# First blocks row by row in written order, residual transposes ahead of norm 2's rows, and a halved last head

## The chip, the cores and the metric

The kernel runs on one core of a Trainium2 chip. The metric is the device time of one execution in microseconds. Engines are named as in the profile: PE (matrix), PEld (its weight loads), DVE (vector), ACT (scalar), POOL, and SP, which only issues DMAs.

## The reference, cut to what matters

A block of a streaming encoder on 512 tokens of width 1024, in float32: an adaptive vector from `c`, a mixer on a normed and modulated input, and a channel sub-layer that retrieves 16 of 16,384 experts for each of 8 heads.

```python
c_act = jax.nn.silu(c)
ada = c_act @ w_ada[l] + b_ada[l]
sh1, sc1, g1, sh2, sc2, g2 = jnp.split(ada, 6, axis=-1)
h = modulate(rmsnorm(x, norm1_g[l]), sh1, sc1)      # h * (1 + scale) + shift
z = h @ w_in[l]                                     # 1024 -> 2560
...                                                 # convolutions and RG-LRU on z
y = jnp.concatenate([head_rmsnorm(y_a, ...), head_rmsnorm(y_b, ...)], axis=-1) @ w_out[l]
x = x + g1[:, None, :] * y
h = modulate(rmsnorm(x, norm2_g[l]), sh2, sc2)
x = x + g2[:, None, :] * peer(h, w_q[l], sub_keys[l], expert_u[l], expert_v[l])
return rmsnorm(x, final_g)
```

`peer` forms `q = h @ w_q`, scores it against 128 keys on each of two halves, takes the top 16 of each and of their sums, and weighs the chosen experts' outputs.

## The kernel before

Everything up to the experts lies transposed: features on partitions, in eight rows of 128 (`xs[:, k, :]`, k = 0 to 7), and 512 tokens along the free axis. A product with a weight matrix goes block by block, 128 output features at a time. Each float32 weight block is split into a high part (`high`, an ACT copy, L76) and a low part (`low`, a DVE subtraction, L81), the modulated input likewise (L214, L215), and `mm3` adds three matmuls for each of the eight rows: high by high (L90), high by low (L91), low by high (L92). A block is thus 24 matmuls into one PSUM tile.

The front. ACT squares the eight rows (L159, L162), DVE adds them up in `sqa` (L164), one set of matmuls with `ones` sums over partitions (`stat`, L154), DVE and ACT form `rstd` (`rsqrt_small`, L111 to L117), and `rows_of` (L172) spreads it over partitions in `ps_rs`. The first third of the adaptive vector comes in four quarters (`ada_quarter`): four loads of 512 KB each (L190), four pieces of matmuls each (L192) into `ps_g`, an ACT copy `row` (L195), two transposes by the identity (L198), and small DVE additions (L203 to L205) that leave shift and scale `A` for two rows. Then these two rows are modulated. `row` 7 is ready only after the fourth quarter. The softplus of `lam` is a run of small DVE operations (L234 to L254). The bulk of the front is not written in order: a scheduler places the instructions on each engine.

The mixer has 20 input blocks in the list `order`; `zblock` loads, splits and multiplies one, and after each block takes one step of `ada_rest`, whose steps are groups of matmuls L134 for the rest of the adaptive vector. The recurrent branch multiplies `xc` with the block-diagonal `bd` (cleared at L261; L331, L333). Blocks live in the PSUM tiles `ps_z` (three buffers) and `ps_g` (two).

Eight w_out blocks follow, each ending in the residual (L388), a square, and, with the last two squares, the sums (L154). In norm 2 the new residual is also written out in token order: `x1_mm` transposes four rows of 128 tokens (L399) into `ps_z`, `x1_out` copies them to `xn` on ACT (L405; two buffers) and stores them (L406, POOL) to `x1d`. Group 0 to 2 are transposed around `rows_of`, the others one in each of the first heads of the q loop. The rows of h come from L434 (DVE), L213, L214 (ACT) and L215; `full2` transposes them too (L423, L425), into `h2n` and `h2b`.

The q loop makes one q block per head, scores it against the keys (L488) and evicts the scores `sc` (L494). On DVE the top-16 search (`early`, L451 to L460) starts with the first scores. Then the u chunks start: expert weights in blocks of 128, split by the same L76 and L81, multiplied into `ps_act` (pool `psE`). From there on the order is written out by hand, by a planner (`manual_schedule`).

Of the kernel before, what the change touches and what calls it, by code (L numbers as in the profile page):

```python
# [34 lines left out]
def block_kernel(ctx, tc, xT, small, w_ada1, w_ada, b_ada, w_in, w_r, w_i, w_out, w_q, keys, uT, u, v, final_g, out):  # L35
# [120 lines left out]

    def sq_sum(k, split):
        if k == 0:
            nc.scalar.activation(sqa, xs[:, 0, :], AF.Square)  # L159
# [25 lines left out]
    def ada_quarter(j):  # L185
        pr = psZ.tile([128, 256], F32, name="ps_g", bufs=2)
        nc.vector.memset(pr, 0.0)
        for k2 in range(4):
# [1 line left out]
            nc.sync.dma_start(wt.rearrange("p a b c -> p (a b c)"), w_ada1[4 * j + k2])  # L190
            for b in range(4):
                nc.tensor.matmul(pr[32 * b:32 * b + 1, :], cs[:, 2 * k2 + b // 2:2 * k2 + b // 2 + 1],  # L192
                                 wt[:, b // 2, b % 2, :], start=(k2 == 0), stop=(k2 == 3), skip_group_check=True)
        row = ada0.tile([128, 256], F32, name="row0", bufs=2)
        nc.scalar.activation(row, pr, AF.Copy)  # L195
        pc = psA.tile([128, 2, 128], F32, name="ps_row")
        for i in range(2):
            nc.tensor.transpose(pc[:, i, :], row[:, i * 128:(i + 1) * 128], ident)  # L198
# [6 lines left out]
        nc.vector.scalar_tensor_tensor(A1[:, ks], adac[:, 8 + 2 * j:10 + 2 * j], 1.0, sm("n1g")[:, ks],  # L205
                                       op0=OP.add, op1=OP.mult)
# [4 lines left out]
    def modulate(t1, k, A, B, hh, hl, full=None):
        f = sq_pool.tile([128, T], F32, name="mfull")
        nc.vector.tensor_scalar(f, t1, A[:, k:k + 1], B[:, k:k + 1], op0=OP.mult, op1=OP.add)  # L213
        nc.scalar.activation(hh[:, k, :], t1, AF.Identity, scale=A[:, k:k + 1], bias=B[:, k:k + 1])  # L214
# [19 lines left out]
    nc.vector.tensor_scalar(z_, lam, -1.0, None, op0=OP.mult)  # L234
    nc.vector.tensor_tensor(z_, z_, lam, op=OP.max)
    nc.scalar.activation(tn, z_, AF.Tanh, scale=1.0 / 16)
    nc.vector.tensor_scalar(e_, tn, 1.0, None, op0=OP.add)
    nc.vector.reciprocal(e_, e_)
    nc.vector.tensor_scalar(tn, tn, -1.0, 1.0, op0=OP.mult, op1=OP.add)
    nc.vector.tensor_mul(e_, e_, tn)  # L240
    for _ in range(3):
        nc.vector.tensor_mul(e_, e_, e_)
    nc.vector.tensor_scalar(w_, e_, 2.0, None, op0=OP.add)
    nc.vector.reciprocal(w_, w_)
    nc.vector.tensor_mul(w_, w_, e_)
    nc.vector.tensor_mul(w2, w_, w_)
    nc.vector.memset(ac, 1.0 / 15)
    for n in range(6, -1, -1):
        nc.vector.tensor_mul(ac, ac, w2)
        nc.vector.tensor_scalar(ac, ac, 1.0 / (2 * n + 1), None, op0=OP.add)  # L250
# [885 lines left out]
```

## Time and profile before

| | us |
|---|---|
| median of three runs | 1416.25 (1416.03, 1416.25, 1418.21) |
| the profiled execution | 1418.33 |
| its span | 1416.6 |

| engine | busy us | share of the span |
|---|---|---|
| PE | 1363.8 | 96% |
| DVE | 1241.4 | 88% |
| ACT | 753.0 | 53% |
| POOL | 497.1 | 35% |

The span runs from the first to the last instruction of the core; the time of an execution has some 2 us around it. A share over the whole span is an average over stages with different limits, so what a change is worth is read in the stage that it touches, by windows and by what each engine waited for there. In rows of instructions the first number is the start in microseconds, the second the time taken, then engine, line, operation, what is written and read, and in brackets the idle time just before with what ended it. The granted clock is that of PE: 1.00 is full speed.

### The profile page before, as it was taken

To read this page: it belongs to the slowest core of one execution; us is meant where nothing else is said; L and a number is where in the kernel's file an instruction comes from. 1 tells how busy PE (TensorE), PEld (TensorE's weight loads), DVE (VectorE), ACT (ScalarE), POOL (GpSimd) and SP (SyncE) were. 2 spreads that over 40 slices of the span, in tenths; PEclk is the share of its full clock that TensorE was granted. 3 is DMA by queue.
4 is the path that set the end of the run, shared out by engine and by line. 5 is a ranking of instruction groups with operands and counts; after the bars stand their busy time and mean duration, and the time that the engine had idled before them with its cause. 6 is when DMAs were issued, how large, how long until landed. Compare 5 with 4: busy or idle time off the path is not lost.

```text
span 1416.6 us, 22503 instructions
## 1 busy us (share of the span) xinstructions
PE 1363.8 (96%) x7739; PEld 1179.4 (83%) x7739; DVE 1241.4 (88%) x2598; ACT 753.0 (53%) x1340; POOL 497.1 (35%) x334
## 2 busy tenths in 40 slices
PE   5999998999999999999999989999999999999995
PEld 2566777779999999999999978876878888888884
DVE  6676555899999899999999967988989999999998
ACT  3554433445498699856995434343344434344442
POOL 0000000000135334415342534655656565555550
PEclk9999999999999999999999989999999999999998
DMA  9575323124689899979999999999999999999994
GB/s 381 207 271 190 119 89 100 57 83 149 213 299 387 314 354 370 388 232 323 353 374 350 339 380 354 381 372 390 391 411 410 412 409 412 405 409 409 406 370 163
DMA packets 160758, 440.13 MB, mean 311 GB/s; under 512 B 16258, under 2 KB 68482, under 8 KB 158596
## 3 DMA queue, kind: packets, MB, share of 16 engines
q1 hardware_dynamic: 113636, 267.76, 51.0%
q0 software_dynamic: 46720, 169.89, 31.3%
q8 instruction: 61, 1.00, 0.3%
q10 hardware_dynamic: 288, 1.05, 0.2%
q14 instruction: 53, 0.43, 0.1%
HBM read 393.54 MB, written 45.09 MB: 310 GB/s over the span
## 4 chain that ended last, share of the span: by engine, by line
PE 43%; issue 21%; DVE 14%; DMA 13%; POOL 6%; ACT 1%; SPq 1%; DVEq 0%; POOLq 0%; ACTq 0%
PE acc L987 18%; POOL rows L730 6%; DMA wraw<-in_v_dram 6%; PE ps_z L90 5%; PE ps_z L92 5%; PE ps_z L91 5%; DVE scr L751 3%; DMA rows<-in_u_dram,idx_s 2%; DVE wlo L81 2%; PE ps_act L90 2%; PE ps_act L92 2%; PE ps_act L91 2%; DVE cl L874 2%; DVE ys L767 1%; DMA act<-Ad 1%
## 5 line engine op out<-in xcount | busy, mean ns | idle before, releaser
L76 ACT ACTIVATE whi<-wraw 128x1024 fp32r<-128x1024 f32 x292 | 308.2, 1056 | 334.3 <-DMA wraw<-in_v_dram 131.9
L81 DVE TENSOR_TENSOR wlo<-wraw,whi 128x1024 fp32r<-128x1024 f32 x292 | 356.1, 1221 | 71.5 <-ACT whi L76 70.6
L90 PE MATMUL ps_act<-h,whi 128*128 128x320 f32 x1024 | 322.4, 315 | 1.6 <-ACT sc L494 1.2
L91 PE MATMUL ps_act<-h,whi 128*128 128x320 f32 x1024 | 317.0, 310 | 0.0
L92 PE MATMUL ps_act<-h,wlo 128*128 128x320 f32 x1024 | 316.8, 309 | 0.0
L730 POOL DMA_INDIRECT rows<-in_u_dram,idx_s x128 | 194.1, 1516 | 239.0 <-DVE scr L751 189.8
L730 POOL DMA_INDIRECT rows<-in_v_dram,idx_s x128 | 198.7, 1552 | 147.0 <-DVE ys L767 119.5
L987 PE MATMUL acc<-whi,ch 128*128 128x512 f32 x750 | 234.3, 393 | 13.0 <-ACT ch L884 6.7
L987 PE MATMUL acc<-whi,cl 128*128 128x512 f32 x750 | 234.3, 394 | 0.4
L987 PE MATMUL acc<-wlo,ch 128*128 128x512 f32 x750 | 233.2, 392 | 0.0
L90 PEld LDWEIGHTS ps_act<-h,whi 128*128 128x128 f32 x1024 | 193.1, 189 | 2.2 <-ACT sc L494 1.4
L91 PEld LDWEIGHTS ps_act<-h,whi 128*128 128x128 f32 x1024 | 193.1, 189 | 0.2
L92 PEld LDWEIGHTS ps_act<-h,wlo 128*128 128x128 f32 x1024 | 192.7, 188 | 0.0
L987 PEld LDWEIGHTS acc<-whi,ch 128*128 128x128 f32 x750 | 141.7, 190 | 44.7 <-ACT ch L884 8.4
L730 POOL DMA_INDIRECT rows<-in_u_dram,idx_b x64 | 99.1, 1548 | 211.7 <-DVE scr L751 109.1
L987 PEld LDWEIGHTS acc<-whi,cl 128*128 128x128 f32 x750 | 141.4, 190 | 33.5 <-DVE cl L874 4.6
L987 PEld LDWEIGHTS acc<-wlo,ch 128*128 128x128 f32 x750 | 142.3, 190 | 29.9
L767 DVE SCALAR_TENSOR_TENSOR ys<-rows,acts,ys 128x1024 f32<-128x1024 f32 x127 | 162.8, 1282 | 1.6
L751 DVE SCALAR_TENSOR_TENSOR scr<-rows,h2n 128x1024 f16<-128x1024 f32 x128 | 156.4, 1222 | 8.3 <-DMA rows<-in_u_dram,idx_s 6.6
L884 ACT ACTIVATE ch<-cf 128x384 fp32r<-128x384 f32 x128 | 67.3, 526 | 93.4 <-DVE cf L881 91.0
L817 ACT ACTIVATE act<-ps_act 128x320 f32<-128x320 f32 x128 | 55.5, 433 | 102.2 <-PE ps_act L92 100.3
L406 POOL DMA_DIRECT2D x1d<-xn x8 | 4.6, 578 | 281.8 <-DVE wlo L81 234.4
(258 smaller groups left out, 1964.7 us busy)
## 6 DMA issues: line engine op xcount, KB each, us to landing
wraw<-in_uT_dram SPq DMA_DIRECT2D x128, 512.0 KB, 6.5
wraw<-in_v_dram SPq DMA_DIRECT2D x128, 512.0 KB, 10.0
Gd<-stg SPq DMA_DIRECT2D x46, 512.0 KB, 6.9
wada<-in_w_ada_dram SPq DMA_DIRECT2D x16, 1024.0 KB, 5.0
Ad<-act SPq DMA_DIRECT2D x96, 160.0 KB, 7.6
act<-Ad SPq DMA_DIRECT2D x96, 160.0 KB, 11.0
h<-Gd SPq DMA_DIRECT2D x12, 1024.0 KB, 14.7
wraw<-in_w_in_dram SPq DMA_DIRECT2D x20, 512.0 KB, 5.8
```

Source lines behind the costliest of these rows:

```text
L76: nc.scalar.activation(hi, raw, AF.Copy)
L81: nc.vector.tensor_sub(lo, raw, hi.bitcast(F32))
L90: nc.tensor.matmul(ps, hi[:, k, :], xh(k), start=first and k == ks[0], stop=False)
L91: nc.tensor.matmul(ps, hi[:, k, :], xl(k), start=False, stop=False)
L92: nc.tensor.matmul(ps, lo[:, k, :], xh(k), start=False, stop=last and k == ks[-1])
L730: nc.gpsimd.indirect_dma_start(out=r[:, :], out_offset=None, in_=table, in_offset=bass.IndirectOffsetOnAxis(ap=idxs[:, k:k + 1], axis=0))
L751: nc.vector.scalar_tensor_tensor(scr, rows.pop(n), 1.0, hn, op0=OP.mult, op1=OP.mult, accum_out=dst[:, k:k + 1])
L767: nc.vector.scalar_tensor_tensor(ys, rows.pop(k), acts[:, k:k + 1], ys, op0=OP.mult, op1=OP.add)
L817: nc.scalar.activation(act[c], ps, AF.Gelu)
L874: nc.vector.tensor_sub(cl, cf, ch.bitcast(F32))
L884: nc.scalar.activation(ch, cf, AF.Copy)
L987: nc.tensor.matmul(accs[b][e], st[:, bs], mv[:, e * 512:(e + 1) * 512], start=first, stop=last)
```

## The change

It has three places. **The front** is put under a written order. The loads come in the order of `FW`. Squares are formed in `xn1`, added in pairs and summed pair by pair. The first quarter of the vector is worked off at once; the pieces of the other three stand in the table `ADA` between matmuls of the blocks. Of the vector's row only the needed columns are picked out, by a matmul with two columns (`selc`) in place of two transposes. The first four blocks no longer run one after the other: for each row k, one of the three products is added in all four blocks, then the next. Softplus is a generator that is advanced between the rows. Blocks 4 and 5 are split between the blocks' last rows.

```diff
+    for what in FW:
+        if what[0] == "p":
+            ada_load(int(what[1]))
+        else:
+            raws[order[int(what[1])]] = load_w(w_in[order[int(what[1])]])
...
+    for k in range(0, KB, 2):
+        for i in range(2):
+            nc.scalar.activation(xn1[:, k + i, :], xs[:, k + i, :], AF.Square)
+        nc.vector.tensor_add(xn1[:, k, :], xn1[:, k, :], xn1[:, k + 1, :])
+        stat(xn1[:, k, :], k == 0, k == KB - 2)
+    for i in range(4):
+        ada_mm(0, i)
+    rstd1 = const.tile([128, NT], F32, name="rstd1")
+    rsqrt_small(rstd1, pst, 1.0 / D, NT)
+    next(soft)
+    rs1 = psA.tile([128, T], F32, name="ps_rs")
+    rows_of(rs1, rstd1)
+    ada_row(0)
+    ada_sel(0)
...
+    for j, part in [(0, 0), (0, 2), (1, 0), (1, 2), (0, 1), (1, 1)] + [(j, e) for j in range(2, KB - 1) for e in range(3)]:
+        if part == 0 and j > 1:
+            mod_high(xn1[:, j, :], j, A1, adac[:, 0:8], h1h)
...
+            mod_low(j, fulls.pop(j), h1h, h1l)
+        for n in order[:4]:
+            nc.tensor.matmul(zps[n], zsp[n][part == 1][:, j, :], (hx, hx, lx)[part](j),
+                             start=j == 0 and part == 0, stop=False)
+        for q, i in ADA.get((j, part), ()):
+            if i < 4:
+                ada_mm(q, i)
+            else:
+                ada_sel(q)
...
+        if j == 0:
+            ada_load(3)
+        elif j < 3:
+            raws[order[3 + j]] = load_w(w_in[order[3 + j]])
+    mod_high(xn1[:, 7, :], 7, A1, adac[:, 0:8], h1h)
+    mod_low(7, fulls.pop(7), h1h, h1l)
+    for i, n in enumerate(order[:4]):
+        mm3(zps[n], *zsp[n], hx, lx, [KB - 1], False, True)
+        if i < 2:
+            zsp[order[4 + i]] = split_w(raws[order[4 + i]])
...
+ADA = {(0, 2): [(1, 0)], (1, 0): [(1, 1)], (1, 2): [(1, 2), (1, 3)], (0, 1): [(1, 4)], (1, 1): [(2, 0), (2, 1)],
+       (2, 0): [(2, 2)], (2, 1): [(2, 3)], (3, 0): [(2, 4)], (3, 1): [(3, 0), (3, 1)], (3, 2): [(3, 2)],
+       (4, 0): [(3, 3)], (4, 1): [(3, 4)]}
+FW = ('p0', 'w0', 'w1', 'w2', 'w3', 'p1', 'p2')
+XE1 = 6
+X1 = ['ps_row', 'ps_g', 'ps_g'] + ['ps_z'] * 3 + ['ps_col', 'ps_z']
```

On PE, from the row sums (L172) on, the order before was (a piece of the vector is a row with `wada0`; numbers tell buffers apart):

```order
L172 MATMUL ps_rs_145<-ident_70,rstd1_135 128x128 x4
L192 MATMUL ps_g_155<-wada0_175,cs_106 1x256 x4
L198 MATMUL ps_row_183<-ident_70,row0_181 128x128 x2
L192 MATMUL ps_g_201<-wada0_203,cs_106 1x256 x4
L90 MATMUL ps_z_392<-h2_82,whi_388 128x512
L192 MATMUL ps_g_201<-wada0_209,cs_106 1x256 x4
L91 MATMUL ps_z_392<-h2_82,whi_388 128x512
L192 MATMUL ps_g_201<-wada0_215,cs_106 1x256 x4
L192 MATMUL ps_g_201<-wada0_221,cs_106 1x256 x4
L198 MATMUL ps_row_229<-ident_70,row0_227 128x128 x2
L92 MATMUL ps_z_392<-h2_82,wlo_390 128x512
L90 MATMUL ps_z_392<-h2_82,whi_388 128x512
```

and is now, from the last piece of the first quarter on:

```order
L228 MATMUL ps_g_117<-wada0_127,cs_106 1x256 x4
L157 MATMUL ps_rs_212<-ident_70,rstd1_198 128x128 x4
L241 MATMUL ps_row_219<-selc_119,row0_217 128x2 x2
L302 MATMUL ps_g_240<-h2_82,whi_230 128x512
L302 MATMUL ps_z_241<-h2_82,whi_232 128x512
L302 MATMUL ps_z_242<-h2_82,whi_235 128x512
L302 MATMUL ps_z_243<-h2_82,whi_238 128x512
L302 MATMUL ps_g_240<-h2_82,whi_230 128x512
L302 MATMUL ps_z_241<-h2_82,whi_232 128x512
L302 MATMUL ps_z_242<-h2_82,whi_235 128x512
L302 MATMUL ps_z_243<-h2_82,whi_238 128x512
L228 MATMUL ps_g_117<-wada0_137,cs_106 1x256 x4
```

Before, single matmuls of one block (`ps_z_392`) stood between the pieces of the first two quarters; now the whole first quarter and the row sums (L157) are done first, and then each step is one matmul for each of four blocks, with a piece of the second quarter behind the second step.

**Norm 2.** The sum of `sqa` moves into the last w_out block, and seven groups of transposes, not three, go ahead of the q blocks, into the PSUM tiles that `X1` names; all seven are copied out ahead of the fifth row of h.

```diff
-        sq_sum(m, True)
+        if m < KB - 1:
+            nc.vector.tensor_add(sqa, sqa, sq)
+        if m >= KB - 2:
+            stat(sqa if m < KB - 1 else sq, m < KB - 1, m == KB - 1)
...
-    x1p = [x1_mm(0)]
     psr2 = psA.tile([128, T], F32, name="ps_rs")
     rows_of(psr2, rstd2)
-    x1p += [x1_mm(1), x1_mm(2)]
+    x1p = [x1_mm(i) for i in range(XE1)]
...
-        if k < 3:
+        if k < XE1:
             x1_out(*x1p[k])
```

On ACT, from the first copy of the residual on, with what each instruction waits for (DMASW are the stores), before:

```order
L405 ACTIVATE xn<-ps_z 128x512 [waits PE_49]
L162 ACTIVATE sq<-xs 128x512 [waits DVE_49,Activation_49]
L405 ACTIVATE xn<-ps_z 128x512 [waits PE_49]
L112 ACTIVATE rs_t<-rs_m 128x4 [waits DVE_49]
L405 ACTIVATE xn<-ps_z 128x512 [waits DMASW0_49,PE_49,Activation_49]
L214 ACTIVATE h_82<-mt_1883,adac,A_1872 128x512 [waits DVE_49]
L214 ACTIVATE h_82<-mt_1897,adac,A_1872 128x512 [waits DVE_49]
L405 ACTIVATE xn<-ps_z 128x512 [waits DMASW1_49,PE_49,Activation_49]
L214 ACTIVATE h_82<-mt_1909,adac,A_1872 128x512 [waits DVE_49]
L214 ACTIVATE h_82<-mt_1921,adac,A_1872 128x512 [waits DVE_49]
```

and now:

```order
L487 ACTIVATE xn<-ps_row 128x512 [waits PE_49]
L466 ACTIVATE sq<-xs 128x512 [waits DVE_49,Activation_49]
L487 ACTIVATE xn<-ps_g 128x512 [waits PE_49]
L112 ACTIVATE rs_t<-rs_m 128x4 [waits DVE_49]
L487 ACTIVATE xn<-ps_g 128x512 [waits DMASW0_49,PE_49,Activation_49]
L487 ACTIVATE xn<-ps_z 128x512 [waits DMASW1_49,PE_49,Activation_49]
L171 ACTIVATE h_82<-mt_1895,adac,A_1884 128x512 [waits DVE_49]
L171 ACTIVATE h_82<-mt_1909,adac,A_1884 128x512 [waits DVE_49]
L487 ACTIVATE xn<-ps_z 128x512 [waits DMASW2_49,PE_49,Activation_49]
L487 ACTIVATE xn<-ps_z 128x512 [waits DMASW3_49,PE_49,Activation_49]
L171 ACTIVATE h_82<-mt_1921,adac,A_1884 128x512 [waits DVE_49]
L171 ACTIVATE h_82<-mt_1933,adac,A_1884 128x512 [waits DVE_49]
```

Two copies behind two stores, not one, stand ahead of the first row of h (L214 before, L171 now), two more ahead of the third, and one ahead of the fifth.

**The end of the q loop.** Head 7 is cut into halves of 256 columns, the first two u chunks are loaded at head 6 and the first is split ahead of head 7, and the pool `psE` releases its tiles one by one.

```diff
+        if h == 6:
+            for k in range(2):
+                wraw[k] = load_w(uT[k])
...
+        if h == 7:
+            whi[0] = high(wraw[0])
+            wlo[0] = low(wraw.pop(0), whi[0])
         qT = qp.tile([128, T], F32, name="qT")
-        nc.scalar.activation(qT, ps, AF.Copy)
+        cuts = [(0, 2), (2, 4)] if h == 7 else [(0, 4)]
+        for a, b in cuts:
+            s = slice(128 * a, 128 * b)
+            mm3(ps[:, s], hi, lo, lambda k: h2h[:, k, s], lambda k: h2l[:, k, s], range(KB), True, True)
+            nc.scalar.activation(qT[:, s], ps[:, s], AF.Copy)
...
-        if h + 3 < 8:
-            x1_out(*x1_mm(h + 3))
+        if h + XE1 < 8:
+            x1_out(*x1_mm(h + XE1))
...
-    psE = psx.enter_context(tc.tile_pool(name="psE", bufs=1, space=PS))
+    psE = psx.enter_context(tc.tile_pool(name="psE", bufs=1, space=PS, reuse_waits="tile"))
```

On PE, from the last matmuls of head 7 to the first u chunk, before:

```order
L90 MATMUL ps_z<-h_82,whi 128x512
L91 MATMUL ps_z<-h_82,whi 128x512
L92 MATMUL ps_z<-h_82,wlo 128x512
L488 MATMUL ps_g<-keys_sb,qT 128x128 [waits Activation_49]
L488 MATMUL ps_g<-keys_sb,qT 128x128 [waits PE_49]
L488 MATMUL ps_g<-keys_sb,qT 128x128 x6
L90 MATMUL ps_act<-h_82,whi 128x320 [waits Activation_49]
L91 MATMUL ps_act<-h_82,whi 128x320
L92 MATMUL ps_act<-h_82,wlo 128x320 [waits DVE_49]
```

and now:

```order
L90 MATMUL ps_z<-h_82,whi 128x256
L91 MATMUL ps_z<-h_82,whi 128x256
L92 MATMUL ps_z<-h_82,wlo 128x256
L582 MATMUL ps_g<-keys_sb,qT 128x128 [waits PE_49] x2
L582 MATMUL ps_g<-keys_sb,qT 128x128 x2
L582 MATMUL ps_g<-keys_sb,qT 128x128 [waits Activation_49]
L582 MATMUL ps_g<-keys_sb,qT 128x128 x3
L90 MATMUL ps_act<-h_82,whi 128x320
L91 MATMUL ps_act<-h_82,whi 128x320
L92 MATMUL ps_act<-h_82,wlo 128x320 [waits DVE_49]
```

The scores' matmuls of the first half wait only for what is long done, those of the second half for its copy (L578), and the first matmul into `ps_act` no longer waits for ACT.

More of the change, by code (lines that the diff above doesn't have):

```diff
@@ L183, in block_kernel @@
     xn1 = ada0.tile([128, KB, T], F32, name="xn1", bufs=1)
[L185 to L188, printed above, removed]
-            wt = ada0.tile([128, 2, 2, 256], F32, name="wada0")
[L190 to L196, printed above, removed]
+    sp = const.tile([128, 4], F32, name="sp")
@@ L197, in ada_quarter, with ada_row, ada_sel @@
+    def ada_row(j):
+        rows0[j] = ada0.tile([128, 256], F32, name="row0", bufs=2)
+        nc.scalar.activation(rows0[j], prs[:, j % 2, :], AF.Copy)
+    def ada_sel(j):
+        pc = psA.tile([128, 2, 2], F32, name="ps_row")
+        row = rows0.pop(j)
         for i in range(2):
-            nc.tensor.transpose(pc[:, i, :], row[:, i * 128:(i + 1) * 128], ident)
-        pcv = pc.rearrange("p i (b r) -> p b i r", r=32)[:, :, :, 0]
+            nc.tensor.matmul(pc[:, i, :], row[:, 128 * i:128 * i + 128], selc, start=True, stop=True)
@@ L234, in block_kernel @@
[L234 to L250, printed above, removed]
-    nc.vector.tensor_mul(ac, ac, w_)
-    nc.vector.tensor_scalar(z_, lam, -1.0, 0.0, op0=OP.mult, op1=OP.max)
-    nc.vector.tensor_scalar(ac, ac, 8.0, None, op0=OP.mult)
-    nc.vector.scalar_tensor_tensor(sp, z_, 4.0, ac, op0=OP.mult, op1=OP.add)
+    rows0, fulls = {}, {}
@@ new lines, in block_kernel @@
+    for i in range(4):
+        ada_mm(0, i)
[6 more added lines that the diff above has]
+    ada_sel(0)
+    nc.vector.tensor_mul(xn1[:, 0, :], xs[:, 0, :], rs1)
+    fulls[0] = mod_full(xn1[:, 0, :], 0, A1, adac[:, 0:8])
+    nc.vector.tensor_mul(xn1[:, 1, :], xs[:, 1, :], rs1)
+    fulls[1] = mod_full(xn1[:, 1, :], 1, A1, adac[:, 0:8])
@@ new lines, in block_kernel @@
+    his = {}
+    for i, n in enumerate(order[:4]):
+        his[n] = high(raws[n])
+        if i == 1:
+            mod_high(xn1[:, 0, :], 0, A1, adac[:, 0:8], h1h)
+        if i == 2:
+            mod_high(xn1[:, 1, :], 1, A1, adac[:, 0:8], h1h)
+    zps = {n: psZ.tile([128, T], F32, name="ps_z" if i else "ps_g", bufs=3 if i else 2)
+           for i, n in enumerate(order[:4])}
+    for i, n in enumerate(order[:4]):
+        zsp[n] = his[n], low(raws[n], his[n])
+        if i < 2:
+            mod_low(i, fulls.pop(i), h1h, h1l)
@@ L470, in block_kernel @@
     qsp = {}
+    wraw, whi, wlo = {}, {}, {}
     early = chain(*(stage1([h], range(NT)) for h in range(HQ)))
@@ L781, in block_kernel @@
             jobs.append(("u", CE + n))
-    wraw, whi, wlo = {}, {}, {}
     v0 = max(CE - RB + 3, 0) // 8 * 8 + 8
```

153 lines of the change are left out of this document (98 added, 55 removed).

## Prediction

> **What bounds the kernel now.** First the page's busy shares, then windows over the span, to see which engine is full in which stage; after that the waits and the timeline at the three places that the change touches.
>
> ```profile
> PE 1363.8 (96%) x7739; PEld 1179.4 (83%) x7739; DVE 1241.4 (88%) x2598; ACT 753.0 (53%) x1340; POOL 497.1 (35%) x334
> ...
> 50.00:60.00 10.00, 10.00 (x48) 5.67 (x47) 6.80 (x12) 8.44 (x12) 0.00 (x0) 1.00 0.63 212
> ...
> 270.00:398.00 128.00, 124.56 (x820) 116.56 (x819) 127.15 (x614) 63.96 (x100) 9.98 (x11) 0.99 0.43 146
> ...
> 398.00:842.00 444.00, 439.13 (x3168) 437.62 (x3167) 411.77 (x906) 338.04 (x657) 175.61 (x111) 1.00 0.94 345
> 842.00:1416.60 574.60, 549.48 (x2400) 450.67 (x2400) 529.54 (x723) 230.93 (x414) 307.86 (x201) 0.98 0.98 381
> ```
>
> The columns of a window are its length, then busy time on PE, PEld, DVE, ACT and POOL, the granted clock, the DMA share and GB/s. PE is the bound from about 29 us on through the mixer (10.00 of 10 from 50 to 60, and 7.80 of 7.80 in a row of part 1). From 270 to 398 DVE is: 127.15 of 128 us, while it runs the expert search and makes the low halves of the weights. After 398 PE is full again (439.13 of 444). So a microsecond gained in the first stage is kept, a microsecond gained ahead of DVE's first search is kept, and one that PE alone gains between 270 and 398 is not.
>
> **Part 1, the front.** The trace before, with PE's stalls and the state in which it had finished four blocks:
>
> ```profile
> 23.00 0.80 PE L90 MATMUL ps_z<-h,whi 128*128 128x512 f32 x1 [1.89 <-ACT h L214]
> ...
> 47.33 0.39 PE L90 MATMUL ps_z<-h,whi 128*128 128x512 f32 x1
> 47.56 0.40 PE L91 MATMUL ps_z<-h,whi 128*128 128x512 f32 x1
> ...
> 62.40 0.39 PE L90 MATMUL ps_z<-h,whi 128*128 128x512 f32 x1
> ...
> 62.85 0.39 PE L92 MATMUL ps_z<-h,wlo 128*128 128x512 f32 x1
> 63.17 1.04 PE L134 MATMUL ps_row<-wada,cs 128*1 128x512 f32 x8
> ...
> 22.40:29.20 6.80, 5.70 (x31) 2.29 (x32) 6.11 (x14) 2.58 (x4) 0.00 (x0) 0.50 1.03 422
> 29.20:37.00 7.80, 7.80 (x54) 3.81 (x53) 3.41 (x6) 2.08 (x4) 0.00 (x0) 1.00 1.02 420
> ```
>
> The spacing of two projection matmuls is 0.23 us (47.33 to 47.56). The four blocks have 4 x 8 x 3 = 96 of them. In PE's order the third group of L134 stands behind the 99th, so the matmuls from 62.40 to 62.85, three at that spacing, are numbers 97 to 99, and the 96th ended at 62.40. By then PE had also done two groups of L134 and the two matmuls on bd, which in the changed order come behind the 96th:
>
> ```profile
> 51.75 1.04 PE L134 MATMUL ps_row<-wada,cs 128*1 128x512 f32 x8
> ...
> 57.46 1.02 PE L331 MATMUL ps_g<-xc,bd 128*128 128x512 f32 x2
> 58.32 1.02 PE L333 MATMUL ps_g<-xc,bd 128*128 128x512 f32 x2
> ...
> 30.21 0.61 PE L192 MATMUL ps_g<-wada,cs 128*1 128x256 f32 x8
> 30.75 0.50 PE L90 MATMUL ps_z<-h,whi 128*128 128x512 f32 x1
> 31.09 0.39 PE L91 MATMUL ps_z<-h,whi 128*128 128x512 f32 x1
> ```
>
> A group of L134 takes 1.04, each of L331 and L333 58.32 - 57.46 = 0.86. So the same work would have been done at 62.40 - 2.1 - 1.7 = **58.6**. That is the number to beat.
>
> After the change PE does, from its first projection matmul on, 96 x 0.23 = 22.1 us, and 12 pieces of the adaptive vector (three quarters of four). A piece takes 0.54 (30.21 to 30.75), and each visit to one costs 0.1 ahead and 0.11 behind (30.75 to 31.09 is 0.34 instead of 0.23); the written order makes nine visits: 12 x 0.54 + 9 x 0.21 = 8.4. Three pairs of selc matmuls are put at 0.3 each, 0.9; the two transposes that a pair replaces took 0.38 (46.19 below). Sum 31.4 with nothing late.
>
> When does it start? The squares are added in pairs, four DVE additions instead of seven, and the sums over partitions begin with the first pair:
>
> ```profile
> 17.01 2.08 PE L172 MATMUL ps_rs<-ident,rstd 128*128 128x128 f32 x8
> 22.13 1.52 ACT L214 ACTIVATE h<-xn,adac,A 128x512 fp32r<-128x512 f32 x2 [1.11 <-DVE A L205]
> 46.19 0.38 PE L198 MATMUL ps_row<-ident,row 128*128 128x128 f32 x2
> 49.88 0.91 DVE L261 MEMSET bd<- 128x1024 f32 x1 [0.16 <-issue]
> ```
>
> The row sums ended at 17.01 + 2.08 = 19.1, yet the first h began at 22.13, after ACT had waited 1.11 for A: DVE had four products and other work in between. After the change a selector (0.3), two small additions and one product lie between; I give them 1.6 us, let the row sums end 0.6 earlier for the additions saved, and keep the 0.87 from h to the first matmul (22.13 to 23.00): 19.1 - 0.6 + 1.6 + 0.9 = **21.0**. Bounds: 23.0 (the first quarter's 16 matmuls now all stand ahead of the row sums in PE's order) and 19.5.
>
> Then what is late. (a) The clock. In the two slices 22.40 to 29.20 it was granted at 0.50, and here one spacing is twice as long; the order after is fuller from 21 on, so I take 5.6 us at half clock, 2.8 lost, with bounds 1 and 4.5. (b) PE is in order, and each step of four waits for its weights' halves and for the row: 0.6 at the start. (c) Ahead of row 7's low half DVE now has the memset of bd, 0.91, which before was covered: 0.9. Together 21.0 + 31.4 + 2.8 + 0.6 + 0.9 = **56.7**, against 58.6: 1.9 won. Behind it the four blocks end within 12 x 0.23 = 2.8 us, where before they were spread over more than ten, and ACT reads them one by one with two splits between; the fifth block waits for a freed ps_z, and L331's matmuls for xc. Two L134 groups (2.1) cover most; I charge 0.4 (0 to 1.5). **Front: 1.5 us won**, from -0.5 to 3.5.
>
> **Part 2, norm 2.**
>
> ```profile
> 233.31 0.94 PE L154 MATMUL ps_col<-ones,sqa 128*128 128x1 f32 x8
> 238.51 1.16 PE L172 MATMUL ps_rs<-ident,rstd 128*128 128x128 f32 x8 [1.50 <-DVE rstd L117]
> 240.52 0.60 ACT L405 ACTIVATE xn<-ps_z 128x512 f32<-128x512 f32 x1 [3.06 <-DMA x1d<-xn]
> 241.01 1.51 ACT L214 ACTIVATE h<-mt,adac,A 128x512 fp32r<-128x512 f32 x2
> ...
> 250.89 1.52 ACT L214 ACTIVATE h<-mt,adac,A 128x512 fp32r<-128x512 f32 x2
> ...
> 263.52 0.48 DVE L451 MAX8 top<-sc 128x8 f32<-128x128 f32 x2
> ...
> 235.71 4.71 DMA x1d<-xn
> ...
> DMA to landing us min/median/max: 2.2/4.3/12.7
> ...
> 237.45:240.86 3.41, 1.16 (x8) 0.97 (x8) 1.99 (x7) 0.35 (x2) 0.00 (x0) 1.00 0.72 245
> 240.86:247.68 6.82, 5.81 (x21) 3.83 (x22) 5.26 (x10) 3.66 (x6) 1.16 (x2) 0.50 0.10 40
> ```
>
> The 0.94 of the first sum moves into the last w_out block: the last block ends that much later, and the sum is out of the way behind it. ACT's xn and sq, which stood between, take up part of that, so I charge 0.6 to the row sums at 238.51. On ACT the third copy waits for the first store (240.52, after 3.06 idle), and the first h comes right behind it, at 241.01. Now the fourth copy, which waits for the second store, stands ahead of that h as well: 0.60 for the copy, 0.6 for the late start and 0.2 for the second store make +1.4 on the first h; later h's stand behind two more pairs of copies, and stores landed 2.2 us after issue at the least and 4.3 in the middle. What is won: the transposes that stood between the q matmuls at half clock go ahead of the row sums; they fill the wait of 1.50 and the window 237.45 to 240.86, which was busy for 1.16 of 3.41 us and was followed by 6.82 us at 0.50. In those PE was busy 5.81, half of which full clock would give back if ACT and DVE kept up. They are late by 1.4 at first, so I take not 2.9 but 2.4 for it, and against the 1.4: **1.0 won** at DVE's first search (263.52). Bounds: 2.4 won (stores land in 2.2) and 2.0 lost (all land in 4.71; worked out with the rivals).
>
> ```profile
> 234.04:237.45 3.41, 2.64 (x22) 2.32 (x22) 1.61 (x3) 2.11 (x5) 1.31 (x2) 1.00 0.29 62
> 234.04:237.45 3.41, 1.51 (x12) 1.35 (x12) 1.00 0.29 62
> ```
>
> These are the window before that one, for all work and for L399's transposes alone. Without the transposes PE was busy 2.64 - 1.51 = 1.13 there, as little as in the next, yet the clock stayed at 1.00 behind it; so the transposes counted. [...]
>
> **Part 3, the end of the q loop.**
>
> ```profile
> 260.95 1.23 DVE L81 TENSOR_TENSOR wlo<-wraw,whi 128x1024 fp32r<-128x1024 f32 x1 [4.50 <-ACT whi L76]
> ...
> 307.15 1.16 PE L488 MATMUL ps_g<-keys_sb,qT 64*128 64x128 f32 x16 [1.41 <-ACT qT L484]
> 309.48 0.63 PE L90 MATMUL ps_act<-h,whi 128*128 128x320 f32 x1 [1.17 <-ACT sc L494]
> ...
> 309.12:312.54 3.42, 3.06 (x11) 3.06 (x12) 3.42 (x26) 0.30 (x1) 0.00 (x0) 0.50 0.40 156
> ...
> 397.78 1.13 PE L622 MATMUL ps_gt<-igh,jh 128*128 128x128 f32 x8 [0.86 <-ACT stg L631]
> ```
>
> Halving head 7 and the finer release of psE take away 1.41 + 1.17 = 2.6 us of stalls, and with them the half clock that follows (309.12 to 312.54, busy 3.06 at 0.50, so another 1.5): PE gains some 4 us there. But from 270 to 398 DVE is idle for 0.85 us in all, its last long wait (4.50) ended at 260.95, and at 397.78 PE already waits 0.86 for what DVE makes. PE would only wait longer there. I count **0.3** (0 to 4). The first chunk's two loads and split move ahead of head 7, onto DMA that is a quarter busy and a DVE that has the split to do anyway: nothing.
>
> **Sum.** 1.5 + 1.0 + 0.3 = 2.8 us. The profiled execution took 1418.33 us with a span of 1416.6, so it would take 1415.5; it is 2.1 above the median, and the median of 1416.25 becomes **1413.4**.
>
> **The rivals.** *The tail counts too:* DVE is not as full as its row says, since the searches can give way to the weights' halves; then PE's 4 us are kept: 1409.4. Against it speaks the 127.15 of 128. *The front gives nothing:* row-by-row order ties PE to the latest of four blocks' operands, the clock stays at half for all of 21 to 28, and blocks that end together queue on ACT; the first projection matmul comes earlier, but the fifth block begins where it did: 1416.25 - 1.3 = 1415.0. For it speaks that DMA is full until 37 us (1.03, 1.02), so that weights cannot come sooner. *Slower, the stores on ACT:* the copies of groups 2 to 5 wait for four stores in pairs, ahead of the h's; it decides once they land over 4 us after issue, as the first did. From the landing of the first store, 0.6 later than the old 240.42, come two rounds of copy (0.60), issue (0.3) and store (4.71), and one more copy: 241.0 + 11.2 + 0.6 = 252.8 for the fifth h, 1.9 behind the old 250.89. The stall leaves another stretch like the 6.82 us at 0.50, whose 5.81 of work lose 2.9; with the front's 1.5 and none of the tail: 1416.25 + 1.9 + 2.9 - 1.5 = 1419.6. Against it: the DMA share there is 0.10, so most stores should land nearer to 2.2.
>
> **How the numbers follow.** The forecast has 0.55 (1411.4 to 1415.4), the tail 0.15, the idle front 0.18, the stores 0.12. A measurement tells about 0.2% from no change, 2.8 us, so faster begins at 1413.4, in the middle of the forecast: faster 0.15 + 0.3 = 0.45, same 0.25 + 0.18 = 0.43, slower 0.12. The range 1409.4 to 1418.6 takes in the bounds of the terms, except both bad ends together, and leaves out about half of the tail's case and most of the stores'.
>
> **What would show it.** The 96th projection matmul ending near 56.7; a granted clock of 1.00 from 26 us at the latest; no wait of the fifth block over half a microsecond. In norm 2 the first h near 242.4 less what the front won, clock 1.00 behind the row sums, and DVE's first search at 263.52 less 2.5. In the tail head 7's two waits gone, and a longer one of PE at L622 near 397 in their place. I am wrong if DVE has idle time between 270 and 398, or if the first search comes no earlier than before.

## The result, and the profile after

The changed kernel took 1436.10 us (median of 4 runs, 1433.02 to 1438.51), the kernel before, measured with it, 1417.23 (1416.03 to 1418.91): a ratio of 1.0136, with a 95% interval of 1.0121 to 1.0152. It is 19 us slower, outside the forecast range. The profiled execution took 1438.51 us, its span 1436.7.

From the page of the changed kernel, the busy shares and two groups (after the count: busy time in us and mean ns of one, then the idle time of the engine just before, and what ended most of it):

```profile
PE 1375.7 (96%) x7795; PEld 1187.2 (83%) x7795; DVE 1238.5 (86%) x2589; ACT 752.5 (52%) x1341; POOL 497.8 (35%) x334
...
L76 ACT ACTIVATE whi<-wraw 128x1024 fp32r<-128x1024 f32 x292 | 308.1, 1056 | 364.6 <-DMA wraw<-in_v_dram 165.5
...
L1079 PE MATMUL acc<-whi,ch 128*128 128x512 f32 x750 | 236.9, 397 | 24.3 <-ACT ch L977 17.2
```

The same two groups of the page of before:

```profile
L76 ACT ACTIVATE whi<-wraw 128x1024 fp32r<-128x1024 f32 x292 | 308.2, 1056 | 334.3 <-DMA wraw<-in_v_dram 131.9
...
L987 PE MATMUL acc<-whi,ch 128*128 128x512 f32 x750 | 234.3, 393 | 13.0 <-ACT ch L884 6.7
```

No instruction has become longer to speak of. What has grown is waiting: ACT's copies of weight blocks wait 33.6 us more for loads of `in_v`, and PE waits 10.5 us more ahead of the output matmuls for `ch`. ACT copies `ch` from `cf`, which DVE for the most part makes from the gates and the activations `act` that are loaded back, and DVE waits longer for these loads. Its waits from 842 us on, before and after (us in all, times, longest):

```profile
DVE cf L881 <- DMA act<-Ad: 9.8, 6, 4.0
```

```profile
DVE cf L974 <- DMA act<-Ad: 19.1, 7, 5.2
```

So both are waits for DMA, in the last stage. Windows of the changed kernel (columns as in the prediction's windows):

```profile
22.40:29.20 6.80, 5.94 (x19) 2.94 (x18) 6.80 (x9) 1.75 (x3) 0.00 (x0) 0.54 1.03 410
270.00:398.00 128.00, 124.42 (x836) 116.62 (x834) 127.33 (x623) 61.88 (x96) 8.36 (x8) 1.00 0.40 137
398.00:842.00 444.00, 439.81 (x3173) 438.13 (x3171) 412.62 (x908) 337.50 (x656) 173.69 (x111) 1.00 0.94 343
...
850.00:1350.00 500.00, 481.41 (x2092) 392.00 (x2091) 443.37 (x590) 195.63 (x342) 279.62 (x182) 0.98 1.02 384
```

and the last of them before:

```profile
850.00:1350.00 500.00, 492.92 (x2175) 405.77 (x2174) 460.94 (x610) 203.47 (x356) 287.73 (x189) 0.99 1.02 398
```

Up to 842 us the two are alike: 439.81 against 439.13 us of PE in the 444. From 850 to 1350 PE does 2092 matmuls instead of 2175, 3.8% fewer, while the DMA share is the same 1.02 and the rate falls from 398 to 384 GB/s. So the DMA engines are busy all the time in both, and deliver 3.5% less. By the starts of the 292 high halves (L76), the changed kernel is 1.3 us late at the 12th, 1.4 at the 144th (754 us), 2.0 at the 160th, 8.8 at the 210th (1059), 14.2 at the 240th and 20.1 at the 282nd (1362): hardly anything up to the place where the DMA is full without a break, then a steady loss.

The edits lie in the first 310 us; what reaches the last stage is something that they leave behind. The program moves the same 160,758 packets and 440.13 MB. But one new tile, `selc`, two floats for each partition, stands in the pool `const`, ahead of the large pools, and takes 32 bytes there. In the built programs every large tile behind it begins 32 bytes later: the ring `wraw`, into which the weights are loaded, at byte 56,864 of a partition instead of 56,832; `rows`, into which POOL gathers, at 106,016 instead of 105,984. The old starts are multiples of 256, the new ones are not. And the packets take longer; worked out from the trace's packets of 4096 bytes, 1010 to 1350 us:

| | gathers (POOL's queue), mean ns | weights (SP's queue), mean ns |
|---|---|---|
| before | 160.5 | 160.3 |
| after | 166.4 | 164.9 |

The median goes from 159 to 165 ns for the gathers and 164 for the weights, 3.8 and 3.1%, about as much as the rate falls. It does so only where the DMA is full: from 398 to 842 us, at 343 GB/s, the median of the 4096-byte packets is 159 ns on both queues in the changed kernel too.

### The profile page after: what moved, and what is told of

Read it like the earlier page. It is cut to its first block, busy times and chain, and to the rows that moved or that the text cites. A ratio compares the mean times of both kernels' runs of the same rounds, so it can differ in the third digit from the quotient of the medians.

```text
span 1436.7 us, 22598 instructions
## 1 busy us (share of the span) xinstructions
PE 1375.7 (96%) x7795; PEld 1187.2 (83%) x7795; DVE 1238.5 (86%) x2589; ACT 752.5 (52%) x1341; POOL 497.8 (35%) x334
## 2 busy tenths in 40 slices
DMA packets 160758, 440.13 MB, mean 306 GB/s; under 512 B 16258, under 2 KB 68482, under 8 KB 158596
## 4 chain that ended last, share of the span: by engine, by line
PE 41%; DVE 24%; DMA 19%; issue 10%; ACT 3%; SPq 2%; DVEq 0%; POOL 0%; ACTq 0%
DMA wraw<-in_v_dram 10%; PE ps_act L91 6%; PE ps_act L90 6%; PE ps_act L92 6%; DVE wlo L81 5%; PE ps_gt L716 5%; PE acc L1079 4%; PE ps_z L90 3%; PE ps_z L92 3%; PE ps_z L91 3%; DVE scr L845 3%; DVE cl L967 2%; DVE ys L861 2%; DMA h<-Gd 2%; ACT whi L76 2%
## 5 line engine op out<-in xcount | busy, mean ns | idle before, releaser
L76 ACT ACTIVATE whi<-wraw 128x1024 fp32r<-128x1024 f32 x292 | 308.1, 1056 | 364.6 <-DMA wraw<-in_v_dram 165.5
L861 DVE SCALAR_TENSOR_TENSOR ys<-rows,acts,ys 128x1024 f32<-128x1024 f32 x127 | 162.6, 1280 | 1.6
L910 ACT ACTIVATE act<-ps_act 128x320 f32<-128x320 f32 x128 | 55.4, 433 | 103.5 <-PE ps_act L92 99.7
L716 PE MATMUL ps_gt<-igh,jh 128*128 128x128 f32 x768 | 97.4, 275 | 3.1 <-ACT igh L708 1.3
```

The source lines that it names most:

```text
L76: nc.scalar.activation(hi, raw, AF.Copy)
L716: nc.tensor.matmul(pg[:, :, k], jh[:, k, :], ig[:, k, :], start=True, stop=True)
L861: nc.vector.scalar_tensor_tensor(ys, rows.pop(k), acts[:, k:k + 1], ys, op0=OP.mult, op1=OP.add)
L910: nc.scalar.activation(act[c], ps, AF.Gelu)
```

## The experiments

Each is compared with the kernel before, run with it on the same chip. First: is it the place of the tiles (theory A: where a DMA lands, 256 bytes decide; A64: 64 bytes do) or the new order (theory B)? The changed kernel with the tiles behind `selc` moved on to the next multiple of 256, and to 64 past one:

```diff
-    selc = const.tile([128, 2], F32, name="selc")
+    selc = const.tile([128, 64], F32, name="selc")[:, 0:2]     # e1_after_o256
+    selc = const.tile([128, 16], F32, name="selc")[:, 0:2]     # e2_after_o64
```

> The changed kernel, with the selector tile widened from 8 to 256 bytes a partition (only 8 used): every tile behind it lies 224 bytes further, so that the weight ring and the gathered rows start at multiples of 256 bytes again, as before the change. No instruction differs. Theory A (the new tile's 32 bytes moved the DMA's targets off their 256-byte boundary): the 4096-byte packets go back from a median of 165 ns to 159 ns in the last stage, and the time falls from 1436 to about 1413 to 1418 us. Theory A64 (only 64-byte boundaries count): the same. Theory B (the new order shifts transfers against each other, and the addresses mean nothing): the time stays at 1433 to 1438, packets at 165.

> The changed kernel, with the selector tile widened to 64 bytes, so that the DMA's targets lie 64 bytes past a multiple of 256. Theory A (256-byte boundaries): still slow, about 1433 to 1440 us, packets at 163 ns or more. Theory A64 (64-byte boundaries): 1413 to 1418 us, packets at 159. Theory B (order): 1433 to 1438 whatever the width.

And the kernel before, with nothing but its tiles moved, 32 and 128 past:

```diff
-    rstd1 = const.tile([128, NT], F32, name="rstd1")
+    rstd1 = const.tile([128, 16], F32, name="rstd1")[:, 0:NT]  # e3_before_o32
+    rstd1 = const.tile([128, 40], F32, name="rstd1")[:, 0:NT]  # e4_before_o128
```

> The kernel before, with one small tile (rstd1) widened so that all tiles behind it lie 32 bytes further; no instruction differs. Theories A and A64: slower by 16 to 20 us, about 1433 to 1437, packets of 4096 bytes at 165 ns in the last stage instead of 159. Theory B (order): no change, 1416 to 1418.

> The kernel before, with the same tile widened so that all tiles behind it lie 128 bytes further. Theory A (256): slower, by an amount between 5 and 20 us. Theory A64 (64): no change, 1416 to 1418. Theory B (order): no change.

| | starts past 256 | us | ratio to before |
|---|---|---|---|
| e1, changed kernel | 0 | 1418.27 | 1.0012 [0.9998, 1.0026] |
| e2, changed kernel | 64 | 1435.53 | 1.0140 [1.0123, 1.0157] |
| e3, kernel before | 32 | 1431.95 | 1.0113 [1.0096, 1.0129] |
| e4, kernel before | 128 | 1431.29 | 1.0101 [1.0084, 1.0118] |

The DMA view from 1000 to 1300 us gives packets, MB and rate. Here are its rows of before, of after, of e1 and of e3, one fence each:

```profile
DMA packets 51204, 122.79 MB, mean 409 GB/s; under 512 B 4293, under 2 KB 27686, under 8 KB 51182
```

```profile
DMA packets 48815, 117.94 MB, mean 393 GB/s; under 512 B 4121, under 2 KB 26110, under 8 KB 48793
```

```profile
DMA packets 50929, 121.98 MB, mean 407 GB/s; under 512 B 4254, under 2 KB 27593, under 8 KB 50907
```

```profile
DMA packets 49123, 118.49 MB, mean 395 GB/s; under 512 B 4160, under 2 KB 26341, under 8 KB 49101
```

The rate goes with the place, not with the order: 409 and 407 where the tiles begin on 256 bytes, 393 and 395 where they don't. The kernel before loses 16 us when its tiles move by 32 bytes, the changed kernel wins 18 back by 248 more unused bytes in `selc`. (e3's 1431.95 is a little under the 1433 to 1437 that A had.) 32, 64 and 128 past cost alike within each order (1.0136 and 1.0140, 1.0113 and 1.0101), and of the starts that were run only multiples of 256 were fast. Odd ones are fast too: in e1, at 1.0012, the ring begins at byte 57,088 and `rows` at 106,240, both odd multiples of 256. A64 and B fall; the loss is shown from both sides. In e1 the median packet took 159 ns again, and the waits of PE ahead of its output matmuls are (line, releaser; us in all, times, longest), in the changed kernel and in e1:

```profile
PE acc L1079 <- ACT ch L977: 17.2, 8, 4.4
```

```profile
PE acc L1079 <- ACT ch L977: 5.5, 4, 1.8
```

Without the 32 bytes the change is worth +2.0 us, within what a measurement can't tell from nothing. The next runs ask why the 2.8 us of the forecast didn't come. All three start from e1. e5 gives the copies of the residual four buffers `xn` in place of two, and transposes four groups ahead, so that no copy waits for a store before the first h:

```diff
-        xn = qp.tile([128, T], F32, name="xn")
+        xn = qp.tile([128, T], F32, name="xn", bufs=4)
-XE1 = 6
-X1 = ['ps_row', 'ps_g', 'ps_g'] + ['ps_z'] * 3 + ['ps_col', 'ps_z']
+XE1 = 4
+X1 = ['ps_row', 'ps_g', 'ps_g'] + ['ps_z'] * 5
```

> The changed kernel with addresses at multiples of 256 bytes as in e1, and in norm 2 four buffers for the copies instead of two and four transposed groups ahead of the rows instead of six, so that no copy ahead of the first h waits for a store. Theory S (the second store holds the first h, and the idle PE falls to half clock): the first h comes at about 241.6 to 242.2 instead of 243.48 in e1, DVE's first search 1.0 to 2.0 us earlier than e1's 263.95, and the time about 1415 to 1418 instead of 1418.3. Rival P (norm 2 is bound by the chain of products and rows on DVE and ACT, whatever the stores do): the first h moves, but the first search stays within 0.4 us of 263.95.

Measured: 1417.68, ratio 1.0010 [0.9994, 1.0026]. The timeline of e5, PE's row sums, the first h and DVE's first search:

```profile
241.57 2.07 PE L157 MATMUL ps_rs<-ident,rstd 128*128 128x128 f32 x8 [1.50 <-DVE rstd L117]
...
244.40 1.52 ACT L171 ACTIVATE h<-mt,adac,A 128x512 fp32r<-128x512 f32 x2 [3.41 <-DVE mt L515]
...
267.08 0.48 DVE L535 MAX8 top<-sc 128x8 f32<-128x128 f32 x2
```

and of e1, with the two copies that wait for stores:

```profile
239.40 1.16 PE L157 MATMUL ps_rs<-ident,rstd 128*128 128x128 f32 x8 [0.24 <-DVE rstd L117]
...
241.43 0.60 ACT L487 ACTIVATE xn<-ps_g 128x512 f32<-128x512 f32 x1 [3.09 <-DMA x1d<-xn]
...
242.99 0.60 ACT L487 ACTIVATE xn<-ps_z 128x512 f32<-128x512 f32 x1 [0.96 <-DMA x1d<-xn]
243.48 1.51 ACT L171 ACTIVATE h<-mt,adac,A 128x512 fp32r<-128x512 f32 x2
```

The edit did what it was to do: the first h follows the start of the row sums by 2.83 us instead of 4.08. (Theory S's 241.6 to 242.2 for it didn't come, since this run began its row sums 2.2 us later.) The search follows it by 25.51 instead of 24.55 all the same (263.95 in e1). So the wait for the stores is there, as forecast, and without it the search comes no sooner. But e5 also does fewer transposes ahead of the row sums (four groups, in e1 seven), and its clock was low for three times as long as e1's, 10.2 us instead of 3.4:

```profile
241.20:251.40 10.20, 8.20 (x30) 5.83 (x31) 6.78 (x14) 3.52 (x5) 1.08 (x2) 0.50 0.38 148
```

```profile
245.40:248.80 3.40, 3.40 (x9) 2.63 (x10) 3.40 (x7) 2.47 (x4) 1.08 (x2) 0.51 0.42 174
```

How much of the 1.25 us the low clock took back, this run can't tell. So rival P (the chain of products on DVE and ACT sets the search, whatever the stores do) isn't shown by it.

e6 takes two of the groups L134, which stood together behind the fourth block, into the row-by-row part, since in e1 a later group waits for its load there:

```diff
+    first = ada_group(1)
...
+        if (j, part) in ((5, 2), (6, 2)):
+            next(first)
...
-        yield from ada_group(1)
+        yield from first
...
-        next(ada_it, None)
+        if n not in order[1:3]:
+            next(ada_it, None)
```

> The kernel of e1, with the first two L134 groups of the adaptive vector put between the blocks' rows 5 and 6, not behind the 96th projection matmul, so that their buffers come free and the third load is issued earlier. Theory L (the front's 2 us were given back because the third load comes late, L134 waits 0.96 for it, and the next groups are pushed into each other): the 0.96 us wait goes, and the second pair of bd matmuls starts 1 to 2 us before e1's 85.52. Rival M (the mixer's own chain gives it back: blocks that end together are read one by one by ACT): it starts within 0.4 us of 85.52.

Measured: 1419.33, ratio 1.0020 [1.0007, 1.0034]. The wait for the load is gone, but two others stand in the stretch, 0.96 us for ACT's `gr` and 0.79 for its `sq`, and the second pair of matmuls on `bd` begins at 87.64, where in e1 it does at 85.52; 1.6 of the 2.1 was there when the first block began (first matmul into `ps_z` at 22.02 against 20.46). No gain: taking the wait for the load away didn't make the stretch shorter.

e7 is e1 with the end of the q loop as it was before: no halves of head 7, the first expert loads and split behind the loop, `psE` released as before.

```diff
-        if h == 6:
-            for k in range(2):
-                wraw[k] = load_w(uT[k])
...
-        cuts = [(0, 2), (2, 4)] if h == 7 else [(0, 4)]
+        cuts = [(0, 4)]
...
-    psE = psx.enter_context(tc.tile_pool(name="psE", bufs=1, space=PS, reuse_waits="tile"))
+    psE = psx.enter_context(tc.tile_pool(name="psE", bufs=1, space=PS))
```

> The kernel of e1 with the end of the q loop as it was before the change (head 7 whole, the first u chunks loaded and split behind it, psE with its old release). Theory D (DVE is the bound from 270 to 398 and takes up whatever PE gains there): the same time as e1 within 0.2%, and the 60th weight block's high half (395.79 in e1) within 0.4 us. Rival T (the tail's PE gain counts): 3 to 4 us slower there.

Measured: 1418.62, ratio 1.0016 [1.0004, 1.0027], against 1.0012 with the new end: nothing, as the full DVE in 270 to 398 said. The 60th high half isn't within 0.4 us of e1's but 1.7 later; the first search, ahead of this edit, was already 1.65 later (265.60).

e8 is the kernel before with a gap of 224 bytes ahead of two tiles that lie 224 past a boundary in both kernels, `act` and `stg`; its 1280-byte packets go there:

```diff
+    sel.tile([128, 56], F32, name="gap")
```

> The kernel before, with a gap of 224 bytes on the right side of the memory, so that the activation and staging tiles (act, stg: 1280-byte and 4096-byte transfers) start at multiples of 256 bytes too, which they did not before. Theory A (each transfer between the chip's memories is slower off a 256-byte boundary): 2 to 6 us faster than before, at most. Rival (only writes of 4096 bytes into the weight ring and the gathered rows matter, and these were on the boundary already): no change, within 0.2%.

Measured: 1415.86, ratio 0.9996 [0.9982, 1.0010]; these packets stay at 55 ns. So the boundary didn't count for every transfer: it was shown for the 4096-byte packets of weights and gathers.

Then the parts of the change by themselves, and the two halves of the place. e9 is e1 with only the front new (norm 2 and the end of the q loop as before); e10 is the kernel before with only these two new, its tiles on 256 bytes. Their edits are the lines of the change.

> The changed kernel at multiples of 256 bytes, with norm 2 and the end of the q loop as before: of the change only the front is left. Theory F (the front by itself does not pay: its 96th matmul comes 0 to 2 us earlier by the phase of the clock, and 2 us are given back by the second pair of bd matmuls): bd's second pair at 85.5 to 87.7, where the kernels with the old front have 85.2 to 86.0; then the old 24.1 to 25.0 us from norm 2's row sums to the first search; 1416 to 1418 us. Rival N (norm 2 is what costs): the same bd times, but 1414 to 1416 us.

> The kernel before with the changed norm 2 and end of the q loop, and the old front (no selector tile, so addresses as before). Theory F: bd's second pair at 85.2 to 86.0, norm 2's row sums 0.6 later than before relative to it (153.9 us instead of 153.3), the first search 25.3 us behind the row sums instead of 24.1 to 25.0: about 1 us later than before, 1416.5 to 1418 us. If norm 2 did what was forecast, the first search comes 1 us earlier, at 262.5, and 1415 us.

Measured: e9 1417.11, 1.0013 [1.0000, 1.0025]; e10 1416.51, 1.0003 [0.9990, 1.0015]. The first search begins at 263.35 and 263.23, before at 263.52: neither part gains anything clear of noise. The five kernels with the new front on 256 bytes (e1, e5, e6, e7, e9) all lie 0.10 to 0.20% above the kernel before, e6 and e7 with their whole intervals, and e10, with the old front, at 0.03%. So the new front may well cost 1 to 3 us.

e11 and e12 are the kernel before with one of the two streams moved 32 past a boundary: in e11 the gathered rows (`rows`, `rows2`, `gt`), in e12 the weight ring and `h2`.

```diff
+    gap = ctx.enter_context(tc.tile_pool(name="gap", bufs=1)).tile([128, 8], F32, name="gap")    # e11, behind the ring
```

```diff
+    gap = ctx.enter_context(tc.tile_pool(name="gap", bufs=1)).tile([128, 56], F32, name="gap")   # e12, behind the ring
-    rstd1 = const.tile([128, NT], F32, name="rstd1")
+    rstd1 = const.tile([128, 16], F32, name="rstd1")[:, 0:NT]
```

> The kernel before with a gap of 32 bytes behind the weight ring: the gathered rows and the loads of Gd start 32 bytes past a multiple of 256, the weight ring stays on it. Theory own (each packet pays for its own target): packets of the software queue (gathers) go from 159 to about 165 ns, those of the weight loads stay at 159; of the 16 us of e3 some 60% here (the gathers are 16140 of 26721 large packets in the last stage): 1424 to 1428 us. [...]

> The counterpart: the weight ring (and h2) 32 bytes past a multiple of 256, the gathered rows and gt on it. Theory own: packets of the hardware queue's 4096 bytes at about 164 ns, the gathers at 159, and 5 to 8 us of the 16: 1421 to 1425 us. [...]

Measured: e11 1426.12, 1.0072 [1.0053, 1.0091]; e12 1425.66, 1.0072 [1.0049, 1.0095], where both together (e3) cost 1.0113. The DMA view of 1000 to 1300 us gives 403 GB/s for each, midway between before and after:

```profile
DMA packets 50353, 121.03 MB, mean 403 GB/s; under 512 B 4232, under 2 KB 27138, under 8 KB 50331
```

```profile
DMA packets 50365, 120.97 MB, mean 403 GB/s; under 512 B 4231, under 2 KB 27173, under 8 KB 50343
```

Each stream costs some 10 us where both cost 16. The mean packet of the gathers took 162.5 ns in e11 and 162.0 in e12, that of the weights 161.2 and 161.4. So a stream that lands beside the boundary slows the other one too: in e11 the weights, which lie on it, by 0.9 ns and the moved gathers by 2.0; in e12 the gathers, which lie on it, by 1.5 and the moved weights by 1.1. And the medians stay at 159 ns in both: in e11, 74% of the gathers, all of them beside the boundary, still took 159. So the start alone doesn't make a packet slow. Neither a cost of each stream's own packets alone (its 1424 to 1428 us for e11 came, but not its 165 ns) nor one that is full with either fits; how it is shared stays open.

## Why the prediction was wrong, step by step

**The step that failed** is in Part 1: the three pairs of matmuls on `selc` "are put at 0.3 each, 0.9", and that is all that the selector costs there. Its tile was never counted. The prediction also read 398 to the end as PE's stage and priced nothing in it, though its own row from 842 on has a DMA share of 0.98 beside a PE busy for 549.48 of 574.60: there the DMA was a bound as well, and the slower packets (164 and 165 ns instead of 159) showed in the time. The runs put the moved tiles at 1.13% in the old order (e3) and, from 1.0136 and e1's 1.0012, at 1.24% in the new one, 16 to 18 us. No rival held this mechanism; the one on the slow side, the stores on ACT, gave 1419.6, and e10, which has those stores, is at 1.0003.

The rest can be read without the 32 bytes, in e1 and in its parts. One slip of the sums: the tail rival's 1409.4 counts the forecast's 0.3 for the tail twice; by its own terms it is 1409.7.

**Front, 1.5 us won: its first half was about right, its second mis-sized.** PE's timeline of e1: the first matmul of a block, the 96th one's end (the start of the row behind it), and what stands from there to the second pair on `bd`:

```profile
20.46 0.80 PE L302 MATMUL ps_g<-h,whi 128*128 128x512 f32 x1 [1.89 <-ACT h L171]
...
56.70 1.90 PE L134 MATMUL ps_row<-wada,cs 128*1 128x512 f32 x16
...
65.58 1.04 PE L134 MATMUL ps_row<-wada,cs 128*1 128x512 f32 x8 [0.96 <-DMA wada<-in_w_ada_dram]
...
75.06 1.02 PE L134 MATMUL ps_row<-wada,cs 128*1 128x512 f32 x2
76.01 1.05 PE L374 MATMUL ps_col<-hind,sq 128*128 128x2 f32 x8
77.00 1.03 PE L134 MATMUL ps_row<-wada,cs 128*1 128x512 f32 x6
...
85.52 1.13 PE L404 MATMUL ps_g<-xc,bd 128*128 128x512 f32 x2
```

and of before:

```profile
76.70 1.04 PE L134 MATMUL ps_row<-wada,cs 128*1 128x512 f32 x8
77.67 1.05 PE L301 MATMUL ps_col<-hind,sq 128*128 128x2 f32 x8
...
85.17 1.12 PE L331 MATMUL ps_g<-xc,bd 128*128 128x512 f32 x2
```

The 96th ended at 56.70, as forecast, but that e1 hits the number is luck: it is the earliest of six runs with this front, which ended it at 58.0 on average (57.51 in e9, 58.18 in the changed kernel as it is, 59.19 in e2). The kernels with the old front reach the same work at 58.5 to 59.4, worked out like the 58.6, so some 1.0 was won on average instead of 1.9. The first matmul came at 20.46 to 22.22 in the six, against the 21.0. From there to the end it took 36.2 to 37.0 us, forecast 35.7: the parts of that sum were sized about right. The low clock is one of them: in each of the six it was 0.50 for 6.8 us (20.1 to 26.9 in e1, with PE busy for 5.58 of them; 21.8 to 28.6 in the changed kernel, 5.94), and two matmuls were 0.43 us apart there instead of 0.23 (23.66 to 24.09 in e1), so that about half of that, by the two spacings 2.6 to 2.8 us, was lost, as forecast, though the clock wasn't back at 1.00 by 26 us as the prediction's sign had it.

What was charged at 0.4, the work behind the 96th, came out at 2.25 in e1. Before, the 22.77 us from 62.40 to 85.17 held 72 block matmuls, four groups of L134 and two of `hind`; two more groups (2.1) and the first pair on `bd` (1.7) make 26.6. In e1 the same work takes 85.52 - 56.70 = 28.82. Of the 2.25, 0.96 is the wait for the load. Another 0.95 is a group of L134 that is cut in two by the matmuls on `hind`: its first two take from 75.06 to 76.01, as long as a whole group of eight before (76.70 to 77.67), and the other six about as much again. Some 0.3 is left. The wait differs between runs (0.53 in e9, 0.30 in the changed kernel, none in e2, which waits 0.4 for `sq` instead); without these waits the stretch is 1.2 to 1.4 us too long in each, where the cut is the same. That the cut costs this is read from the rows and was not tried by itself; e6, which has no cut and no wait for the load, met other waits instead. With the 1.9 won up to the 96th in e1, and less elsewhere, the second pair on `bd` begins at 85.52 to 87.64 in the six, 86.6 on average, and at 85.09 to 85.99 with the old front, 85.6 on average: nothing won and perhaps 1 us lost. The rival "the front gives nothing" had this outcome, though it put the loss at the fifth block.

**Norm 2, 1.0 won: the wait there and 0.8 longer than forecast, the gain not there.** The first h was to come 1.4 later behind two stores: from the start of the row sums to it there were 2.50 us before, 3.3 by forecast (1.4, less 0.6 for the later row sums), and 4.08 in e1, where the rows above show waits of 3.09 and 0.96 us. Windows of e1 around it:

```profile
237.50:241.00 3.50, 2.81 (x23) 2.38 (x22) 1.41 (x7) 0.20 (x1) 0.57 (x1) 1.00 0.84 281
241.00:244.40 3.40, 0.73 (x6) 0.40 (x6) 1.88 (x5) 2.01 (x4) 1.12 (x2) 1.00 0.26 101
244.40:247.80 3.40, 3.40 (x12) 2.48 (x13) 3.39 (x6) 2.75 (x5) 1.10 (x3) 0.64 0.36 148
```

The transposes do fill the window of the row sums (2.81 us busy instead of 1.16), and the clock behind it is 1.00 where it was 0.50, as forecast. But now PE idles for 2.7 us while ACT waits for the stores, and the low clock comes one window later, when the q matmuls run: 0.64. It lasts 3.4 us in e1 and e10, but 6.8 in the changed kernel (243.7 to 250.5), as long as before. The 2.4 us put down to the clock were for the most part moved, not won. The first search, forecast 2.5 us earlier, came at 263.95 in e1, 265.38 in the changed kernel and 263.23 in e10, against 263.52. That it came no earlier than before, in e1 and the changed kernel, is one of the prediction's own signs of being wrong. Its reading that the transposes counted for the clock fits e9, where norm 2 is the old one: they made up 3.12 of the 3.40 us from 243.0 to 246.4, at 0.50, and behind that the clock was 1.00.

**The tail, 0.3: right.** Head 7's waits shrank but did not go; PE's waits at the end of the loop in e1:

```profile
302.66 0.38 PE L90 MATMUL ps_z<-h,whi 128*128 128x256 f32 x1 [0.53 <-ACT qT L578]
307.09 0.71 PE L582 MATMUL ps_g<-keys_sb,qT 64*128 64x128 f32 x8 [0.66 <-ACT qT L578]
```

1.2 us in place of 2.6. DVE stayed full (127.33 of 128 in the window above), and PE gave the gain back, so that it was busy for 124.42 us of that window, before for 124.56: by one wait of 1.5 us for ACT's `act` (L910), and at the first chunk's transposed gates, in the changed kernel:

```profile
397.37 1.13 PE L716 MATMUL ps_gt<-igh,jh 128*128 128x128 f32 x8 [0.51 <-ACT igh L708]
399.36 0.91 PE L716 MATMUL ps_gt<-igh,jh 128*128 128x128 f32 x6 [0.86 <-DVE jh L700]
```

Undoing this part (e7) changes nothing, so the rival "the tail counts too" falls. In e7 head 7's waits are 1.41 and 1.17 us again, and the clock was 1.00 behind them: the 1.5 us of the half clock don't hang on these waits alone.

**In sum:** of the 2.8 us nothing was won; without the moved tiles the change is at 1.0012, some 1418 us, inside the range of 1409.4 to 1418.6 but not where the forecast was, 1411.4 to 1415.4. The tiles, which the prediction didn't look at, add 18 us. None of the kernels run beat the one before clear of noise.

## What to carry to other kernels

When a change adds a tile, however small (here 32 bytes cost 16 to 18 us), look where the tiles behind it begin: pad it, or put it behind those that DMAs write. (Here padding was tried, putting it behind was not.) Where the DMA share is near 1 and the loss is spread evenly over a stage that the edit doesn't touch, compare the GB/s of that stage and the time of one packet before looking for a cause in the order. And time that an early stage wins on one engine is won only if the work behind it is not then held by the next operand or the next dip of the clock.

## What the runs showed that was not expected

- Weights and gathers that land 32, 64 or 128 bytes past a multiple of 256 in each partition took a median of 162 to 165 ns per 4096-byte packet instead of 159, where the DMA is full: 393 to 395 GB/s instead of 407 to 411, and 1.0 to 1.4% of the whole kernel. The medians rose by 3.1 to 3.8% at 32 past (e3: 165 and 164 ns) and by no more at 128 (e4: 164 and 162), and below a full DMA not at all (159 ns from 398 to 842 us, at 343 GB/s in the changed kernel).
- 1280-byte packets that lie 224 past a boundary gained nothing when they were put on one (55 ns in both), and packets of a stream on the boundary got slower on average (by 0.9 to 1.5 ns) when the other stream left it.
- The same front, in the same order, had its first block matmul anywhere from 20.46 to 22.22 us and ended its 96th between 56.70 and 59.19, in the order in which its stretch of half clock began, at 20.1 to 23.5 us.
